# Mixer B of a two-layer decoder: splitting the projections of its last unit by halves and merging its first half one head later

## The chip, the cores and the metric

The kernel runs on one core of one Trainium2 chip. The metric is the device time of one execution in microseconds (us); lower is better. The core has a matrix engine (TensorE, PE), a vector engine (VectorE, DVE), a scalar engine (ScalarE, ACT), GpSimd (POOL), and SyncE (SP), which here issues nearly all DMA transfers.

## What is computed

A decoder trunk on 1024 tokens and 1024 features, in float32. Layer 1 is a forgetting attention and a convolutional feed-forward net (FFN). Layer 2, which the change is about, is a dilated sliding-window attention ("mixer B") in three dilation groups of eight heads, merged by softmax weights, an output projection and a second FFN; a last norm ends it. The reference, cut to layer 2:

```python
q = (h @ b_w_q[bl]).reshape(B, S, B_N_GROUPS, B_HEADS_PER_GROUP, B_HEAD_DIM)
outs, lses = [], []
for g, (window, dil) in enumerate(B_GROUPS):        # dilations 1, 4, 16
    o_g, lse_g = dilated_branch(q[:, :, g], kv[:, :, 0, g], kv[:, :, 1, g], dil, slopes[g])
    outs.append(o_g)
    lses.append(lse_g)
alpha = jax.nn.softmax(jnp.stack(lses, axis=0), axis=0)
o = jnp.sum(alpha[..., None].astype(outs[0].dtype) * jnp.stack(outs, axis=0), axis=0)
x = x + o.reshape(B, S, B_OUT_WIDTH) @ b_w_out[bl]
h = rms_norm(x, ffn_norm_g[layer])
x = x + conv_ffn(h, ffn_w_up[layer], ffn_conv_w[layer], ffn_conv_b[layer], ffn_w_down[layer])
```

## The kernel before

Every float32 operand of a matmul is a pair: a rounded high part (`yh`, `wh`, written by ACT) and the rest (`yl`, `wl`, written by DVE by a subtraction). `mm3` makes three matmuls of each product (L116 to L118). Tokens are handled in two halves of 512; `hf` or `m` is the number of the half. Weights come by DMA into `wraw` (L89), ACT makes `wh` (L94), DVE makes `wl` (L95).

Mixer B has 12 units: for each of the four head pairs p = 0..3 the groups g = 2, 1, 0. A unit's attention (`attend_b`) goes over m = 0, 1 and the two heads j = 0, 1: scores on PE (L477, L478), a softmax whose first pass is on DVE (L257: it writes `t`, and the row minimum into `st`) and whose exponential is on ACT (L262), transposes (L234) into `tp`, copied as the pair `pt` by ACT and DVE, and the products with v (L247) into `po`, added into `og` by DVE (L272). `values` of one cell (m, j) stands behind `scores_b` of the next cell.

`weave` mixes a unit's attention with a filler: the v, q and k projections of the next unit (`tasks_b`), which are matmuls with nothing of the attention in them. The last unit (p = 3, g = 0; unit 11) has no next unit. Its filler is the output projection of half 0, `out_proj`, and only from the moment on at which half 0 has been merged and stands in `yh`, `yl` (`placed`).

The merge of the three groups needs the softmax statistics of all three with tokens on the partitions. Group 0's are there already, in `st`. For the others `spread` transposes `st` on PE (L536) and stores the rows to DRAM (L548): for group 1 in four DMAs of 1024 separate 4-byte elements each. `stats_by_token` reads them back into `stats` (L599, two DMAs). With both, `each_half(m)` of unit 11 computes the weights (`weigh`: L560 `mn`, L561, L563, ACT L564, then L566 to L569), spreads them over features by PE (L616), scales and adds the groups (`merge_b`: L625 to L627) and splits the sum into `yh`, `yl` (`out_half`).

At the start of unit 11, `reload` brings the merged halves of p = 0..2 from DRAM into `yh`, `yl` (L650, L651) and the residual stream into `xT` (L653): six plus eight DMAs of 256 KB for each half. Then `out_proj` adds into `xT` (L667), and the FFN of half 0 begins: squares and their sum (ACT L175, DVE L177 into `cg` for half 0, `T2h` for half 1), column sums on PE (L185), the norm (PE L198, DVE L207, which writes eight normed pieces), their split into `yh` and `yl` (L152, L153), and the up matmuls (L817).

The order of the work is not that of the program text: the kernel is built under `TileContext(nc, schedule_with_timeline_sim=True)`, a scheduler that orders each engine's instructions, the DMAs on SP's queue among them, by a simulated time. Each engine then runs its list in that order and waits at an instruction until its operands are there. SP's DMAs are dealt to eight lanes, and a DMA waits until the one eight earlier has landed.

Of the kernel before, what the change touches and what calls it, by code (L numbers as in the profile page):

```python
# [8 lines left out]
F32 = mybir.dt.float32  # L9
F32R = mybir.dt.float32r  # L10
# [6 lines left out]
P = 128  # L17
S = 1024
D = 1024
KD = D // P  # L20
KH = KD // 2
NB = S // P
H2 = 512
# [7 lines left out]
NG = len(DILS)  # L31
# [3 lines left out]
RATIO_B = 2.0  # L35
# [15 lines left out]
def trunk(ctx, tc, x, a_w_in, a_b_f, a_w_out, b_w_q, b_w_out, kv_norm_g, w_kv,  # L51
          mix_norm_g, ffn_norm_g, ffn_w_up, ffn_conv_w, ffn_conv_b, ffn_w_down,
          final_norm_g, out):
    nc = tc.nc
# [67 lines left out]
        sl = half(hf)  # L122
        yield from mm3(ps, [(w[k], (yh[:, k, sl], yl[:, k, sl])) for k in range(len(w))])

    def stream(tasks):

        w = None
        for i, (load, body) in enumerate(tasks):
            w = w or load()
            ahead = tasks[i + 1][0]() if i + 1 < len(tasks) else None  # L130
            yield from body(w)
            w = ahead

# [3 lines left out]

    def weave(main, filler, ratio, ready=lambda: True):

        due = 0.0  # L140
        done = False
        for c in main:
            due = due + c * ratio if ready() else 0.0
            while due > 0 and not done:
                f = next(filler, None)
                done = f is None
                due -= f or 0
        while not done:
            done = next(filler, None) is None

# [267 lines left out]
        d = DILS[g]  # L418
        return lambda t: t if d == 1 else t.rearrange("p (r t) -> p r t", r=d // 2)

    def project_v_b(vT, v, g, ptr, w, banks):
        for hf in range(2):
            src, dst = by_residue(g, hf)
            ps = banks(hf)
            yield from project(ps, w, hf)
            nc.scalar.copy(dst(vT), src(ps))
            yield 0
        for b4 in range(2):
            tp = ptr.tile([P, H2], F32, name="tp")
            for b in range(4):  # L430
                nc.tensor.transpose(tp[:, b * P:(b + 1) * P],
                                    vT[:, (4 * b4 + b) * P:(4 * b4 + b + 1) * P], ident)
            dst = v[:, 4 * b4:4 * b4 + 4]
            split(dst[:, :, :, 0:64], dst[:, :, :, 64:P],
                  tp.rearrange("p (b j d) -> p b j d", b=4, j=2))

    def project_q_b(heads, g, w, banks):
        for hf in range(2):
            src, dst = by_residue(g, hf)
            ps = banks(hf)  # L440
            yield from project(ps, w, hf)
            for j, (s1, m1, m2) in enumerate(heads):
                pj = src(ps[64 * j:64 * j + 64])
                nc.scalar.activation(dst(s1[0:64]), pj, AF.Copy, scale=-0.125)
                nc.vector.scalar_tensor_tensor(out=dst(s1[64:P]), in0=pj, scalar=-0.125,
                                               in1=dst(s1[0:64]).bitcast(F32),
                                               op0=ALU.mult, op1=ALU.subtract)
            yield 0

    def project_k_b(heads, g, w, banks):  # L450
        for hf in range(2):
            src, dst = by_residue(g, hf)
            ps = banks(hf)
            yield from project(ps, w, hf)
            for j, (s1, m1, m2) in enumerate(heads):
                split(dst(m1[0:64]), dst(m2[0:64]), src(ps[64 * j:64 * j + 64]))
            yield 0
        for s1, m1, m2 in heads:
            nc.vector.tensor_copy(m1[64:P], m1[0:64])
            nc.vector.tensor_copy(m2[64:P], m2[0:64])  # L460

    def scores_b(ap, psc, p, g, j, head, st, m):

# [22 lines left out]
            yield 4 * P  # L486
        return cell

    def attend_b(ap, ps_, p, g, heads, v, og, st, each_half):
        psc, ptr, pov = ps_  # L490

        def values(m, j, cell):
            js = slice(64 * j, 64 * j + 64)
            po = pov.tile([P, H2], F32, name="po")
            f = 4 * m
            if g == 0:
                opening = [(f, f), (f + 2, f + 2)]
                adding = [(f + 1, f + 1), (f + 3, f + 2)]
                banks = [opening, adding] + ([[(f - 1, f)]] if m else [])
            else:  # L500
                banks = [[(f + 2 * i, f + 2 * i), (f + 2 * i + 1, f + 2 * i)] for i in range(2)]
            for bi, bank in enumerate(banks):
                groups = [(kb, (q - f) * P, [cell.get((kb, q)), cell.get((kb, q + 1))])
                          for kb, q in bank]
                yield from transposed_pv(ap, ptr, po, lambda kb: v[:, kb, j],
                                         (bi == 0, bi == len(banks) - 1), groups)
            add_parts(in_order(g, og[js], m), residues(g)(po))
            if j:
                each_half(m)

        waiting = None
        for m in range(2):
            for j in range(2):
                cell = yield from scores_b(ap, psc, p, g, j, heads[j], st, m)
                if waiting:
                    yield from values(*waiting)
                waiting = (m, j, cell)
        yield from values(*waiting)
# [112 lines left out]
    placed = []  # L631
# [10 lines left out]
        for i, t in enumerate(parts):  # L642
            nc.sync.dma_start(o_sp[k, i][:, sl], t.bitcast(F32))

    def reload(xT, n):

        for hf in range(2):
            sl = half(hf)
            for k in range(n):
                nc.sync.dma_start(yh[:, k, sl].bitcast(F32), o_sp[k, 0][:, sl])  # L650
                nc.sync.dma_start(yl[:, k, sl].bitcast(F32), o_sp[k, 1][:, sl])  # L651
            for d in range(KD):
                nc.sync.dma_start(xT[:, d, sl], x_sp[d][:, sl])  # L653
# [6 lines left out]
                yield d  # L660
                d += 1

    def out_proj(w_out, hf, xT):
        def body(d, w):
            ps = pmm.tile([P, H2], F32, name="mm")
            yield from project(ps, w, hf)
            nc.vector.tensor_tensor(out=xT[:, d, half(hf)], in0=ps, in1=xT[:, d, half(hf)],  # L667
                                    op=ALU.add)
            yield 0
        return stream([(lambda d=d: load_cols(w_out, d * P), lambda w, d=d: body(d, w))  # L670
                       for d in range(KD)])

# [328 lines left out]
    with ExitStack() as st:  # L1003
        psc = pool(st, "psc", bufs=3, space=PSUM)
        ptr = pool(st, "ptr", bufs=2, space=PSUM)
        pov = pool(st, "pov", space=PSUM)
        ps_ = (psc, ptr, pov)
        hp_r = pool(right, "heads_ar", side="right")
        vp = pool(st, "va")
        NP = A_HEADS // 2  # L1010
        heads, vals = {}, {}
# [33 lines left out]
        with ExitStack() as s0:  # L1045
# [7 lines left out]
            with ExitStack() as s1_:  # L1053
# [69 lines left out]
                first = tokens_in(0)  # L1123
# [11 lines left out]
                second = tokens_in(1)  # L1135
# [72 lines left out]
        for u in range(NP):  # L1208
            if u == NP - 1:
                right.close()  # L1210
                xT = pool(right, "xA", side="right").tile([P, KD, S], F32, name="xT")
                reload(xT, u)
                filler = out_proj(a_w_out[0], 0, xT)
            v = [vals[u // 2, hf][u % 2] for hf in range(2)]
            weave(attend_a(ap, ps_, u, heads[u], v, u == NP - 1), filler, RATIO_A,
                  lambda: u < NP - 1 or (u, 1) in placed)
# [36 lines left out]
    with ExitStack() as st:  # L1253
# [26 lines left out]
        def tasks_b(i):  # L1280
# [3 lines left out]
            def banks(n):  # L1284
                def bank(hf):
                    if i == 0 and n + hf in (1, 2):
                        return psc.tile([P, H2], F32, name="sc")
                    return pmm.tile([P, H2], F32, name="mm")
                return bank

            def v(w):
                vT = vtp.tile([P, S], F32, name="vT")
                vals[i] = ap.tile([P, NB, 2, P], F32R, name="v", bufs=2)
                yield from project_v_b(vT, vals[i], g, ptr, w, banks(0))

            def q(w):
                hp = hp_l if i % 2 else hp_r
                heads[i] = [[hp.tile([P, S], F32R, name=f"{n}{j}") for n in ("s1", "m1", "m2")]
                            for j in range(2)]
                yield from project_q_b(heads[i], g, w, banks(1))  # L1300

            def k(w):
                yield from project_k_b(heads[i], g, w, banks(2))

            def by_halves(ws):

# [14 lines left out]
                     lambda: load_cols(wkv, base, gain=g_kv)]  # L1321
            if i == 0:
                return [(lambda: [ld() for ld in loads], by_halves), (lambda: True, end)]
            return list(zip(loads, (v, q, k))) + [(lambda: True, end)]

        by_token = []
        due = []
        filler = stream([t for i in range(len(units)) for t in tasks_b(i)])
        while next(filler) is not None:
            pass  # L1330
        for i, (p, g) in enumerate(units):
            last = i == len(units) - 1
            if g == 2:
# [38 lines left out]
            if last:  # L1372
                right.close()
                xT = pool(right, "xB", side="right").tile([P, KD, S], F32, name="xT")
                reload(xT, p)
                placed.clear()
                filler = out_proj(b_w_out[0], 0, xT)
            weave(attend_b(ap, ps_, p, g, heads[i], vals[i], ogs[g], st, each_half),
                  filler, RATIO_B, lambda: not last or (p, 1) in placed)

    with ExitStack() as st:
        for hf, fp, mm, y3 in after_mixer(st, 1, b_w_out[0], xT):
# [31 lines left out]
```

## Time and profile before

| | us |
|---|---|
| median of 3 runs | 2649.62 (2649.51 to 2653.08) |
| the profiled execution, its own time | 2652.28 |
| its span, first to last instruction | 2650.5 |
| PE busy in the span | 2571.4 (97%) |
| DVE busy in the span | 1949.0 (74%) |
| ACT busy in the span | 1336.9 (50%) |
| mean granted TensorE clock | 0.989 of full speed |

The profiled execution is 2.66 us above the median of the runs. Times in the trace count from the start of the span. The stretch that the change touches lies between about 1850 and 1960 us, from the end of unit 10 to the start of the second FFN. A busy time adds up what an engine executed; instructions overlap a little on DVE and ACT, so a group's mean duration is somewhat above the distance from one start to the next.

### The profile page before, as it was taken

What the parts mean: (1) busy time and instruction counts of PE and PEld (TensorE: products, weight loads), DVE (VectorE), ACT (ScalarE), POOL (GpSimd) and SP (SyncE); (2) the same over time, 40 slices, a digit from 0 to 9 for tenths busy, and PEclk for the clock granted to TensorE, in tenths of its full rate; (3) what the DMA queues carried; (4) which work ended last, traced back from release to release, by engine and by line L of the source; (5) the groups of instructions that cost most, each with busy time, mean ns of one, the idle gap of its engine ahead of it and who ended that gap; (6) DMA issues with size and microseconds to landing.
All of it is one profiled execution on the core that took longest, in us unless ns stands there. A gap on an engine that the chain in (4) does not pass through costs nothing.

```text
span 2650.5 us, 36941 instructions
## 1 busy us (share of the span) xinstructions
PE 2571.4 (97%) x12756; PEld 2146.7 (81%) x12756; DVE 1949.0 (74%) x3837; ACT 1336.9 (50%) x2825; POOL 535.7 (20%) x617
## 2 busy tenths in 40 slices
PE   7999999999999999999989999999889999999998
PEld 5898888787788888888778888888677888888887
DVE  6677777677976767778866666767698777777787
ACT  6555656554543434444445565656545444444444
POOL 0222222210112211212132122211011211211121
PEclk9999999999999999999989999999999999999999
DMA  5121211523111111111412323232621111121113
GB/s 185 50 65 49 58 50 50 203 72 108 40 54 50 48 56 48 55 57 44 141 48 33 60 55 58 57 58 56 146 87 48 50 54 49 56 60 52 48 48 116
DMA packets 287380, 180.51 MB, mean 68 GB/s; under 512 B 47728, under 2 KB 263512, under 8 KB 287192
## 3 DMA queue, kind: packets, MB, share of 16 engines
q1 hardware_dynamic: 287080, 178.12, 24.5%
q8 instruction: 101, 1.65, 0.3%
q14 instruction: 87, 0.71, 0.1%
q10 hardware_dynamic: 112, 0.02, 0.0%
HBM read 149.96 MB, written 23.94 MB: 66 GB/s over the span
## 4 chain that ended last, share of the span: by engine, by line
PE 84%; DVE 7%; DMA 4%; ACT 3%; issue 2%; SPq 1%; POOL 0%; POOLq 0%; ACTq 0%; DVEq 0%
PE up L817 30%; PE mm L117 13%; PE mm L116 13%; PE mm L118 13%; PE po L247 4%; PE tp L234 3%; DVE u L768 1%; PE sc L357 1%; DVE t L257 1%; PE sc L358 1%; DMA wb<-wt 1%; DMA stat<-srow 1%; PE up L116 1%; PE up L117 1%; PE up L118 1%
## 5 line engine op out<-in xcount | busy, mean ns | idle before, releaser
L116 PE MATMUL mm<-yh,wh 128*128 128x512 f32 x960 | 380.7, 397 | 8.8 <-ACT yh L152 6.0
L117 PE MATMUL mm<-yl,wh 128*128 128x512 f32 x960 | 381.3, 397 | 0.5 <-DMA yl<-o_sp 0.5
L118 PE MATMUL mm<-yh,wl 128*128 128x512 f32 x960 | 379.6, 395 | 0.0
L152 ACT CAST wh<-wraw 128x512 fp32r<-128x512 f32 x228 | 140.9, 620 | 353.3 <-PE up L817 306.5
L922 DVE TENSOR_TENSOR xT<-mm,xT 128x512 f32<-128x512 f32 x320 | 217.9, 684 | 106.1 <-PE mm L118 104.4
L153 DVE TENSOR_TENSOR wl<-wraw,wh 128x512 fp32r<-128x512 f32 x228 | 169.5, 749 | 150.3 <-ACT wh L152 150.0
L817 PE MATMUL up<-yh,wh 128*128 128x512 f32 x704 | 274.4, 390 | 0.9 <-ACT wh L152 0.9
L817 PE MATMUL up<-yl,wh 128*128 128x512 f32 x704 | 274.1, 389 | 0.0
L817 PE MATMUL up<-yh,wl 128*128 128x512 f32 x704 | 269.0, 389 | 0.0
L117 PE MATMUL mm<-ml,wh 128*128 128x512 f32 x576 | 225.3, 391 | 1.4 <-DVE ml L153 1.4
L116 PE MATMUL mm<-mh,wh 128*128 128x512 f32 x576 | 224.7, 390 | 0.0
L118 PE MATMUL mm<-mh,wl 128*128 128x512 f32 x576 | 223.9, 389 | 0.0
L116 PEld LDWEIGHTS mm<-yh,wh 128*128 128x128 f32 x960 | 181.0, 189 | 44.3 <-ACT yh L152 6.6
L118 PEld LDWEIGHTS mm<-yh,wl 128*128 128x128 f32 x960 | 181.5, 189 | 34.7
L247 PE MATMUL po<-pt,v 128*128 128x256 f32 x1040 | 197.0, 293 | 11.4 <-DVE pt L153 9.7
L117 PEld LDWEIGHTS mm<-yl,wh 128*128 128x128 f32 x960 | 181.5, 189 | 32.7 <-DMA yl<-o_sp 0.7
L153 DVE TENSOR_TENSOR pt<-tp,pt 128x128 fp32r<-128x128 f32 (+2 forms) x408 | 170.7, 433 | 48.3 <-ACT pt L152 43.6
L152 ACT CAST pt<-tp 128x128 fp32r<-128x128 f32 (+2 forms) x408 | 149.6, 382 | 109.5 <-PE tp L234 63.2
L247 PEld LDWEIGHTS po<-pt,v 128*128 128x128 f32 x1040 | 157.3, 192 | 31.5 <-DVE pt L153 13.0
L95 DVE TENSOR_TENSOR wl<-wraw,wh 128x512 fp32r<-128x512 f32 x176 | 129.8, 740 | 69.0 <-ACT wh L94 61.7
L801 POOL TENSOR_TENSOR sraw<-fraw 128x512 f32<-128x512 f32 x40 | 64.8, 1621 | 562.0 <-DMA fraw<-in_ffn_w_up_dram 360.9
L817 PEld LDWEIGHTS up<-yh,wh 128*128 128x128 f32 x704 | 132.1, 188 | 29.8 <-ACT wh L152 1.8
(352 smaller groups left out, 6079.9 us busy)
## 6 DMA issues: line engine op xcount, KB each, us to landing
wraw<-in_ffn_w_down_dram SPq DMA_DIRECT2D x104, 256.0 KB
fraw<-in_ffn_w_up_dram SPq DMA_DIRECT2D x88, 256.0 KB
wraw<-in_ffn_w_up_dram SPq DMA_DIRECT2D x88, 256.0 KB
wraw<-in_a_w_in_dram SPq DMA_DIRECT2D x60, 256.0 KB
wraw<-in_w_kv_dram SPq DMA_DIRECT2D x48, 256.0 KB
wraw<-in_a_w_out_dram SPq DMA_DIRECT2D x32, 256.0 KB
xT<-x_sp SPq DMA_DIRECT2D x32, 256.0 KB
wraw<-in_b_w_q_dram SPq DMA_DIRECT2D x24, 256.0 KB
```

The lines of the kernel that those rows point to most:

```text
L95: nc.vector.tensor_tensor(out=wl, in0=raw, in1=wh.bitcast(F32), op=ALU.subtract)
L116: nc.tensor.matmul(ps, ah, bh, start=(i == 0), stop=False)
L117: nc.tensor.matmul(ps, ah, bl, start=False, stop=False)
L118: nc.tensor.matmul(ps, al, bh, start=False, stop=(i == n - 1))
L152: nc.scalar.copy(h, src)
L153: return nc.vector.tensor_tensor(out=l, in0=src, in1=h.bitcast(F32), op=ALU.subtract).ins
L234: nc.tensor.transpose(tp[:, i * P:(i + 1) * P], c, ident)
L247: nc.tensor.matmul(po[:, col:col + 2 * P], v(kb), pt[:, hl, i * 2 * P:(i + 1) * 2 * P], start=(first and i == 0 and hl == 0), stop=(last a ...
L257: nc.vector.tensor_tensor_reduce(out=t[:, a:b], in0=sc, in1=m, scale=1.0, scalar=INIT if ci == 0 else nm[ci - 1], op0=ALU.add, op1=ALU.min ...
L801: nc.gpsimd.tensor_tensor(out=raw[n], in0=raw[a], in1=raw[b], op=op)
L817: nc.tensor.matmul(ps[bank], a[:, c], b[:, k], start=(start and k == 0 and i == 0), stop=(k == KH - 1 and i == 2), skip_group_check=True)
L922: nc.vector.tensor_tensor(out=xT[:, d, sl], in0=ps, in1=xT[:, d, sl], op=ALU.add)
```

## The change

Only unit 11 and what is woven into unit 10 and unit 11 are touched.

- The three projections of unit 11 are made by halves. Half 0 stays woven into unit 10; half 1 becomes the filler of unit 11's own first half. A marker `NEED` makes `weave` finish that filler ahead of the scores of m = 1.
- `each_half(0)` of unit 11, the merge of half 0, is called after the values of cell (1, 0); before, it was after those of (0, 1).
- `reload` brings half 0 at the start of unit 11 and half 1 behind the marker.
- `out_proj` loads its first weights ahead of its first matmul (`loads_first`), then yields `WAIT` until half 0 is placed.
- v of the second half is staged in a `wb` tile in place of `vT`; the duplicates of k are copied by halves (eight copies of 64x512 in place of four of 64x1024).

The diff, cut to this (lines in the changed file are 19 to 26 later in the functions concerned: L560 becomes L586, L548 L574, L599 L625, L616 L642, L653 L679, L257 L276, L153 L172, L272 L291):

```diff
     def weave(main, filler, ratio, ready=lambda: True):
-        due = 0.0
-        done = False
+        due, met, done = 0.0, 0, False
         for c in main:
+            if c is NEED:
+                while not met:
+                    met = next(filler) is NEED
+                continue
             due = due + c * ratio if ready() else 0.0
             while due > 0 and not done:
                 f = next(filler, None)
+                if f is WAIT:
+                    due = 0.0
+                    break
                 done = f is None
-                due -= f or 0
+                due -= 0 if f is NEED else f or 0
+                met += f is NEED
...
-            nc.vector.tensor_copy(m1[64:P], m1[0:64])
-            nc.vector.tensor_copy(m2[64:P], m2[0:64])
+            nc.vector.tensor_copy(m1[64:P, sl], m1[0:64, sl])
+            nc.vector.tensor_copy(m2[64:P, sl], m2[0:64, sl])
...
             add_parts(in_order(g, og[js], m), residues(g)(po))
-            if j:
+            if last and m > j:
+                each_half(0)
+            if j and m >= last:
                 each_half(m)
         waiting = None
         for m in range(2):
+            if last and m:
+                yield NEED
             for j in range(2):
...
+            if i == len(units) - 1:
+                ws = []
+                def first(f):
+                    def body(w):
+                        ws.append(w)
+                        yield from f(w, (0,))
+                    return body
+                def second(_):
+                    for f, w in zip((v, q, k), ws):
+                        yield from f(w, (1,))
+                return (list(zip(loads, map(first, (v, q, k)))) +
+                        [(lambda: True, f) for f in (end, second, end)])
...
+        def last_filler(rest, p):
+            yield from take(rest)
+            yield NEED
+            reload(xT, p, 1)
+            sums = out_proj(b_w_out[0], 0, xT, loads_first=True)
+            yield next(sums)
+            while (p, 1) not in placed:
+                yield WAIT
+            yield from sums
...
-                reload(xT, p)
+                reload(xT, p, 0)
                 placed.clear()
-                filler = out_proj(b_w_out[0], 0, xT)
-            weave(attend_b(ap, ps_, p, g, heads[i], vals[i], ogs[g], st, each_half),
-                  filler, RATIO_B, lambda: not last or (p, 1) in placed)
+                filler = last_filler(filler, p)
+            weave(attend_b(ap, ps_, p, g, heads[i], vals[i], ogs[g], st, each_half, last),
+                  filler, RATIO_B)
```

What the scheduler makes of it at three places (numbers behind a name tell buffers apart; `x4` is four in a row).

On DVE, around the first instruction of the merge of half 0, `mn<-st,stats`. Before:

```order
L257 ISA t_18747,st_17692<-sc_18744,bias_18736 128x256
L257 ISA t_18753,st_17692<-sc_18750,bias_18736 128x256
L257 ISA t_18759,st_17692<-sc_18756,bias_18736 128x256
L153 TENSOR_TENSOR pt_18764<-tp_18763,pt_18764 128x512
L257 ISA t_18796,st_17692<-sc_18793,bias_18791 128x256
L560 TENSOR_TENSOR mn_18846<-st_17692,stats_18131 128x8
L257 ISA t_18802,st_17692<-sc_18799,bias_18791 128x256
```

And of the change:

```order
L276 ISA t_18671,st_17692<-sc_18668,bias_18642 128x256
L479 COPY m11_18363<-m11_18363 64x512
L480 COPY m21_18364<-m21_18364 64x512
L586 TENSOR_TENSOR mn_18926<-st_17692,stats_18131 128x8
L291 TENSOR_TENSOR og1_18214<-po_18543,og1_18214 64x2x256
L172 TENSOR_TENSOR pt_18679<-tp_18678,pt_18679 128x512
L587 TENSOR_TENSOR mn_18926<-mn_18926,stats_18131 128x8
L276 ISA t_18787,st_17692<-sc_18784,bias_18782 128x256
L172 TENSOR_TENSOR pt_18697<-tp_18696,pt_18697 128x256
L276 ISA t_18819,st_17692<-sc_18816,bias_18782 128x256
L95 TENSOR_TENSOR wl_19127<-wraw_19125,wh_19126 128x512
```

The instruction that waits for `stats` stands ahead of the `pt` of cell (0, 0) and ahead of all softmaxes of m = 1 (buffers 18782 and up); before, it stood behind the last softmax of m = 0, that `pt` and one softmax of m = 1. Soon behind it now comes a `wl` of an output weight, `wraw_19125`.

On SP, from the DMAs of `xT` ahead of the stores of the statistics. Before:

```order
L653 DMA xT_18681<-x_sp_76 128x512 x3
L548 DMA stat3_83<-srow_18601 1024x1x1 x4
L653 DMA xT_18681<-x_sp_76 128x512 x3
L599 DMA stats_18131<-stat3_83 128x16x1 x2
L650 DMA yh_88<-o_sp_77 128x512
L651 DMA yl_89<-o_sp_77 128x512
L653 DMA xT_18681<-x_sp_76 128x512 x8
L89 DMA wraw_19140<-in_b_w_out_dram 128x4x128
```

And of the change:

```order
L679 DMA xT_18590<-x_sp_76 128x512 x11
L574 DMA stat3_83<-srow_18576 1024x1x1 x4
L676 DMA yh_88<-o_sp_77 128x512
L677 DMA yl_89<-o_sp_77 128x512
L625 DMA stats_18131<-stat3_83 128x16x1 x2
L676 DMA yh_88<-o_sp_77 128x512
L677 DMA yl_89<-o_sp_77 128x512
L679 DMA xT_18590<-x_sp_76 128x512 x5
L89 DMA wraw_19125<-in_b_w_out_dram 128x4x128
```

(Of the pairs of `yh` and `yl` each is shown once: before there are three behind `stats`; in the change two stand ahead of `stats` and one behind.) The stores stay behind most of the `xT` transfers, and the first output weight behind the reload is still behind all of it.

On ACT, where the weight that follows the reload is used. Before:

```order
L262 ACTIVATE t_18932,st_17692<-t_18932,st_17692 128x256
L152 CAST yh_88<-og0_18675 128x512
L152 CAST pt_19014<-tp_19013 128x512
L152 CAST pt_19032<-tp_19031 128x256
L564 ACTIVATE ew_19077<-ew_19077 128x3x8
L94 CAST wh_19141<-wraw_19140 128x512
```

And of the change:

```order
L171 CAST pt_18679<-tp_18678 128x512
L171 CAST pt_18697<-tp_18696 128x256
L281 ACTIVATE t_18671,st_17692<-t_18671,st_17692 128x256
L94 CAST wh_19126<-wraw_19125 128x512
L281 ACTIVATE t_18787,st_17692<-t_18787,st_17692 128x256
L171 CAST pt_18697<-tp_18696 128x128
L281 ACTIVATE t_18819,st_17692<-t_18819,st_17692 128x256
L590 ACTIVATE ew_18928<-ew_18928 128x3x8
```

Before, the cast of that weight stood behind the merged `yh` and all exponentials but few; now it stands ahead of the exponentials of m = 1 and of the merge's own (`ew_18928`).

## Rows read from the trace of the kernel before

**Rows 1.** The page: the span, and the busy time of the two busiest engines

```profile
span 2650.5 us, 36941 instructions
PE 2571.4 (97%) x12756; PEld 2146.7 (81%) x12756; DVE 1949.0 (74%) x3837; ACT 1336.9 (50%) x2825; POOL 535.7 (20%) x617
```

**Rows 2.** Windows of the stretch by stage; the first line names the columns

```profile
core 0: us, PE busy (x) PEld busy (x) DVE busy (x) ACT busy (x) POOL busy (x), PEclk, DMA share, GB/s
1858.24:1886.82 28.58, 20.36 (x113) 16.59 (x111) 14.63 (x38) 12.78 (x35) 1.69 (x5) 0.95 0.70 97
1886.82:1902.45 15.63, 11.88 (x59) 9.11 (x59) 13.06 (x51) 10.18 (x31) 1.19 (x4) 0.76 0.91 286
1902.45:1924.91 22.46, 22.44 (x109) 18.76 (x110) 18.66 (x40) 11.47 (x24) 0.00 (x0) 1.00 0.33 98
1924.91:1954.30 29.39, 22.11 (x103) 17.90 (x101) 26.90 (x46) 20.18 (x35) 3.15 (x2) 0.91 0.46 141
1954.30:1959.72 5.42, 5.03 (x11) 3.38 (x11) 5.42 (x11) 0.13 (x1) 4.68 (x1) 0.55 0.00 0
```

**Rows 3.** Waits in 1850 to 1990: us in total, times, longest

```profile
DVE mn L560 <- DMA stats<-stat: 7.7, 1, 7.7
PE po L247 <- DVE pt L153: 7.5, 1, 7.5
PE up L817 <- DVE yl L153: 7.3, 1, 7.3
```

**Rows 4.** The chain that ended last: start, us, what

```profile
1866.60 15.56 DMA stat<-srow
1882.24 4.49 DMA stats<-stat
...
1895.83 4.05 DMA wraw<-in_b_w_out_dram
```

**Rows 5.** Timeline of SP's DMA issues: start, us, line, transfer, count

```profile
1860.09 9.09 SPq L548 DMA_DIRECT2D stat<-srow  x4
1869.22 7.05 SPq L653 DMA_DIRECT2D xT<-x_sp  x3
1882.24 3.44 SPq L599 DMA_DIRECT2D stats<-stat  x2
...
1889.21 5.53 SPq L653 DMA_DIRECT2D xT<-x_sp  x8
1895.15 1.73 SPq L89 DMA_DIRECT2D wraw<-in_b_w_out_dram  x3
```

**Rows 6.** DMA in 1448 to 1476, 40 slices of 0.7 us, and its statistics stores

```profile
GB/s 256 31 0 0 0 0 0 2 2 3 2 2 1 2 1 1 1 1 1 2 0 0 0 7 74 43 44 41 40 59 20 38 77 296 58 217 135 0 0 30
...
1451.45 6.49 SPq L548 DMA_DIRECT2D stat<-srow  x4
```

**Rows 7.** Timeline of PE: start, us, line, tiles, count, idle before and its releaser

```profile
1858.24 0.27 PE L536 MATMUL sc<-ident,st 128*32 128x128 f32 x1
...
1902.47 0.73 PE L116 MATMUL mm<-yh,wh 128*128 128x512 f32 x2 [0.18 <-ACT yh L152]
...
1954.95 0.63 PE L817 MATMUL up<-yh,T3l 128*128 128x512 f32 x1
1955.38 0.63 PE L817 MATMUL up<-yh,T3h 128*128 128x512 f32 x1
```

**Rows 8.** Timeline of DVE: durations, and distances from start to start

```profile
1875.71 1.08 DVE L272 TENSOR_TENSOR og<-po,og 64x512 f32<-64x512 f32 x1 [0.70 <-ACT og L271]
...
1877.03 0.42 DVE L257 CUSTOM_DVE_ANT_0 t<-sc,bias 128x256 f32<-128x256 f32 x1
...
1877.38 0.42 DVE L257 CUSTOM_DVE_ANT_0 t<-sc,bias 128x256 f32<-128x256 f32 x1
...
1878.07 0.69 DVE L153 TENSOR_TENSOR pt<-tp,pt 128x512 fp32r<-128x512 f32 x1
1878.67 0.41 DVE L257 CUSTOM_DVE_ANT_0 t<-sc,bias 128x256 f32<-128x256 f32 x1
```

More of the change, by code (lines that the diff above doesn't have):

```diff
@@ L123, in project, with take, stream @@
         yield from mm3(ps, [(w[k], (yh[:, k, sl], yl[:, k, sl])) for k in range(len(w))])
-    def stream(tasks):
+    NEED, WAIT = object(), object()
+    def take(gen):
+        for c in gen:
+            if c is None:
+                return
+            yield c
+    def stream(tasks, loads_first=False):
         w = None
@@ L130, in stream @@
             ahead = tasks[i + 1][0]() if i + 1 < len(tasks) else None
+            if loads_first and i == 0:
+                yield 0
             yield from body(w)
@@ L419, in residues, with project_v_b @@
         return lambda t: t if d == 1 else t.rearrange("p (r t) -> p r t", r=d // 2)
-    def project_v_b(vT, v, g, ptr, w, banks):
-        for hf in range(2):
+    def project_v_b(vT, v, g, ptr, w, banks, hfs=(0, 1)):
+        for hf in hfs:
             src, dst = by_residue(g, hf)
@@ L427, in project_v_b @@
             yield 0
-        for b4 in range(2):
+        for b4 in hfs:
             tp = ptr.tile([P, H2], F32, name="tp")
@@ L435, in project_v_b, with project_q_b @@
                   tp.rearrange("p (b j d) -> p b j d", b=4, j=2))
-    def project_q_b(heads, g, w, banks):
-        for hf in range(2):
+    def project_q_b(heads, g, w, banks, hfs=(0, 1)):
+        for hf in hfs:
             src, dst = by_residue(g, hf)
@@ L448, in project_q_b, with project_k_b @@
             yield 0
-    def project_k_b(heads, g, w, banks):
-        for hf in range(2):
+    def project_k_b(heads, g, w, banks, hfs=(0, 1)):
+        for hf in hfs:
             src, dst = by_residue(g, hf)
@@ L457, in project_k_b @@
             yield 0
+        sl = slice(hfs[0] * H2, (hfs[-1] + 1) * H2)
         for s1, m1, m2 in heads:
-            nc.vector.tensor_copy(m1[64:P], m1[0:64])
-            nc.vector.tensor_copy(m2[64:P], m2[0:64])
+            nc.vector.tensor_copy(m1[64:P, sl], m1[0:64, sl])
+            nc.vector.tensor_copy(m2[64:P, sl], m2[0:64, sl])
     def scores_b(ap, psc, p, g, j, head, st, m):
@@ L487, in scores_b, with attend_b @@
         return cell
-    def attend_b(ap, ps_, p, g, heads, v, og, st, each_half):
+    def attend_b(ap, ps_, p, g, heads, v, og, st, each_half, last):
         psc, ptr, pov = ps_
@@ L643, in emit_o, with reload @@
             nc.sync.dma_start(o_sp[k, i][:, sl], t.bitcast(F32))
-    def reload(xT, n):
-        for hf in range(2):
+    def reload(xT, n, *hfs):
+        for hf in hfs:
             sl = half(hf)
@@ L661, in blocks_done, with out_proj @@
                 d += 1
-    def out_proj(w_out, hf, xT):
+    def out_proj(w_out, hf, xT, loads_first=False):
         def body(d, w):
@@ L670, in out_proj @@
         return stream([(lambda d=d: load_cols(w_out, d * P), lambda w, d=d: body(d, w))
-                       for d in range(KD)])
+                       for d in range(KD)], loads_first)
     PLAIN = 2
@@ L1211, in trunk @@
                 xT = pool(right, "xA", side="right").tile([P, KD, S], F32, name="xT")
-                reload(xT, u)
+                reload(xT, u, 0, 1)
                 filler = out_proj(a_w_out[0], 0, xT)
@@ L1289, in banks, with v, q, k @@
                 return bank
[L1291 to L1303, printed above, removed]
+            def v(w, hfs=(0, 1)):
+                if hfs[0]:
+                    vT = ap.tile([P, NG, H2], F32, name="wb", bufs=2) \
+                        .rearrange("p g t -> p (g t)")
+                else:
+                    vT = vtp.tile([P, S], F32, name="vT")
+                    vals[i] = ap.tile([P, NB, 2, P], F32R, name="v", bufs=2)
+                yield from project_v_b(vT, vals[i], g, ptr, w, banks(0), hfs)
+            def q(w, hfs=(0, 1)):
+                if not hfs[0]:
+                    hp = hp_l if i % 2 else hp_r
+                    heads[i] = [[hp.tile([P, S], F32R, name=f"{n}{j}")
+                                 for n in ("s1", "m1", "m2")] for j in range(2)]
+                yield from project_q_b(heads[i], g, w, banks(1), hfs)
+            def k(w, hfs=(0, 1)):
+                yield from project_k_b(heads[i], g, w, banks(2), hfs)
             def by_halves(ws):
```

## The prediction, made before the changed kernel was timed

> **What bounds the kernel now.** I began with the page. PE is busy 97% of the span and DVE 74% [rows 1], so over the whole PE is the bound and only stretches where PE stands still can be won. The windows by stage show that such a stretch lies where the change is. I count from X, the transpose of unit 10's statistics at 1858.24 [rows 7], to 1959.72, from where the second FFN runs without a gap. In these 101.48 us PE is busy 81.8 and DVE 78.7 [rows 2]; the reader should see that DVE is the busier of the two from 1886.82 to 1902.45 (13.06 of 15.63) and after 1924.91 (26.90 of 29.39, then all of 5.42). PE's idle time is there because it waits for DVE: the waits show two large stops of PE, 7.5 us for a `pt` and 7.3 us for the first `yl` of the FFN, and one of DVE, 7.7 us for `stats` [rows 3]. The chain shows what is behind the first: 15.56 us of the stores of the statistics and 4.49 us of their reading back, one behind the other [rows 4]. SP's timeline gives the times: stores issued from 1860.09 (X+1.9) to 1869.18, reading back issued at 1882.24 (X+24.0, call this S), `mn` at 1886.82 (X+28.6) [rows 2, 5].
>
> So after `mn` the end of the stretch is set by DVE's list and its waits. I make a ledger: time from X to the end of the stretch = DVE's work + DVE's idle time. Before it is 78.67 + 22.81; the idle time is 13.95 ahead of `mn`, then 2.57, 3.80, 2.49 and 0 [rows 2].
>
> **The change part by part.**
>
> *Work.* PE gets the same products. DVE's list is the same but for four more copies (eight of 64x512 for four of 64x1024). Bounded by nothing (half the length, twice the count) and by the step of a 512-column operation, 0.60 from one start to the next [rows 8], this is 0 to 2.4 us; the half-length copy is nearest to half of it, so I take 0.3 each, about +1: 79.7 us of DVE work. The half-unit of projections is moved, not saved: PE's busy time falls nowhere.
>
> *The filler ahead of the wait.* The 24 k, 2 q and 18 output matmuls of 512 columns and the attention beside them are about 15 us of PE work behind X, at 0.21 each for the matmuls (109 in 22.44 us [rows 2]). That is what the change was to lay over the first stop. It can't shorten the stop: what ends it is the landing of `stats`, and PE reaches the end of its filler at about X+15, well ahead of S.
>
> *The landing of `stats`.* The stores still stand on SP behind most of the `xT` transfers (11 in a row ahead of them, where before five were spread over two places), and wait for the lane of one of those. Before they began at X+1.9 and were down 22.1 us later [rows 5]. They are small but slow by themselves: the same stores of another pair, with hardly a load beside them, moved 1 to 3 GB/s for 13 slices of 0.7 us, up to about 1462, some 11 us behind the start of their issue at 1451.45 [rows 6]. I bound S by X+13 (1.9 + 11) and X+25, and take X+24, that of the row with the same neighbours, since the stores again have a queue of 256 KB transfers ahead of them.
> The Trainium skill, "DMA: Bandwidth & Descriptors", section "Anatomy of one DMA — SWDGE (gpsimd path)", fits a DMA as about 2 us and a term by bytes, next to nothing for 4 KB. By that fit the stores would be down 2 us behind their issue, and the sum would be that of the rival "the cover works" below; the trace does not agree, with 13.1 us from the end of the issue at 1869.18 to 1882.24 [rows 5].
>
> *The first wait moves ahead in DVE's list.* That is the heart of it. The merge of half 0 is one head later in the program, yet its first instruction `mn` now stands ahead of the `pt` of cell (0, 0) and of every softmax of m = 1. Ahead of it DVE has behind X eight softmax passes at 0.34, six operations of 512 columns at 0.60, one add of 1.08 [rows 8], three short ones at some 0.2 and four half copies at 0.3: 9.2 us, with what it has in hand at X some 10.8, where before 14.63 were done [rows 2]. So DVE arrives at about X+12.5 and stands still for 16 us, not 7.7; with it every softmax, `pt` and exponential of m = 1, and PE behind these. `mn` itself comes at S + 4.6, X+28.6, as before; the work not done ahead of it lies behind it: 79.7 - 10.8 = 68.9 us, where before it was 64.0.
>
> *A second wait.* `wraw_19125`, an output weight, is on SP behind the rest of the reload, and its cast on ACT stands ahead of the exponentials of m = 1, its `wl` on DVE early behind `mn`. Reading back takes 3.44 of issue; the two transfers and five `xT` behind it go at 0.69 each (8 in 5.53); so it is issued at S+8.3, and lands 4.05 later [rows 4, 5], S+12.3; ACT's cast and so `wl` follow at about S+12.9, X+36.9. DVE would be there 3.1 us after `mn` (one add of 1.08, one operation of 0.60, four softmax-sized ones at 0.34), X+31.7. It waits 5.2 us. Between 0 (the weight lands with the reload's first pieces) and 8 I keep 5.2. Queued behind it are the softmaxes of m = 1 on DVE and three exponentials and the merge's own on ACT.
>
> *Other idle time of DVE* behind `mn` was 8.86 (2.57 + 3.80 + 2.49). Where DVE stands, ACT and PE catch up, so some of it goes. Bounds: 2.5 and 8.9; I take 5.5.
>
> *The stop at the FFN.* The column sums and norm of half 0 come sooner after the last output sum, and twelve up matmuls can start. But behind these PE waits for the squares of half 1 (`T2h`), at the end of the same DVE list; the 7.3 us stop moves a few matmuls on. I give it nothing of its own; the ledger holds it.
>
> *Ahead of X* PE has two more projection matmuls and three transposes, less four of v: +0.4. *Clock.* After the first stop the granted clock is 0.76 over the next 15.63 us, after the second 0.55, a matmul then taking 0.43 in place of 0.21 [rows 2, 7]; 11 of them cost about 2.4. A longer stop makes one more such start; most of it lies beside DVE's work. Between 0 and 2.4 I take 1.
>
> *Sum.* 28.6 (to `mn`) + 68.9 + 5.2 + 5.5 = 108.2 against 101.5: +6.7; with 0.4 and 1: **+8.1**. The profiled execution took 2652.28, so 2660.4 on it; it stands 2.66 above the median of the runs, so about **2657.7** against that median.
>
> **Rivals.**
>
> *One wait only.* The weight lands early, or DVE's order leaves slack: then 5.2 goes, and with the lower other idle time 3 more: -0.1 to +2.9. For it: three weights are loaded ahead now, and DVE's time there is a sum of small things. Against: SP's order puts the load behind the reload. 2649.5 to 2652.5, no change that can be told.
>
> *The stores land sooner.* With S at X+13 to X+20 all moves ahead by 4 to 11: -3 to +4, 2646.6 to 2653.6. For it: rows 6 show 11 us where little else is loaded. Against: rows 5 show 22.1 us with a load like that of the change.
>
> *The cover works, and it is faster.* Were the four stores down as soon as they are issued, at X+11 (1.9 + 9.09) or, unloaded, X+8.4 (1.9 + 6.49) [rows 5, 6], `mn` would come at X+13 to X+15.6, just when DVE gets there. With 14 for it the ledger gives 14 + 68.9 + 5.2 + 5.5 = 93.6, or -6.5 with the 0.4 and 1: 2643.1; without the second wait 2637.9. It decides from S below about X+10, or X+16 if the second wait goes too. For it: the order on PE does lay 15 us of filler there. Against it: the 15.56 us of the chain in which nothing but the stores is waited for [rows 4].
> It is also what the page of the Trainium skill named above would give.
>
> *Longer.* Other idle time stays at 8.9, and the second weight in line waits too: +12 to +14, 2661.5 to 2664.
>
> **How the numbers follow.** The forecast (both waits, 2654.5 to 2661) has 0.50, longer 0.10, one wait 0.17, sooner 0.12, cover 0.11. The range from 2647 to 2664 takes in the bounds of the single costs, and leaves out most of the cover case and the ends of the others. A measurement of this kernel tells from no change about 0.2%, 5.3 us, so 2644.3 and 2654.9. Slower by more: the forecast but for its lowest end, and longer, 0.58. Faster by more: most of the cover, with a little for a sum that is wrong elsewhere, 0.12. The same: 0.30.
>
> **What would show it.** Right: DVE's wait for `stats` at `mn` of 15 to 17 us from about X+12.5; a wait of ACT or DVE for an output weight of some 5 us soon after; the output projection going on at X+54 (before X+44.2, at 1902.47 [rows 7]); a stop of PE of some 6 us after the first twelve up matmuls. Wrong, if the reading back is issued before X+20, if DVE's idle time from X on stays under 25 us, or if PE has no stop at the FFN at all: then the ledger's work behind `mn` is not what ends the stretch.

## The result, and the profile after

The change is slower: its time is 1.006 of the kernel before (95% interval 1.0047 to 1.0073), 12 to 19 us. The median is 2667.98 us (2663.82 to 2668.84, 4 runs) beside 2650.46 (4 runs); the profiled execution took 2668.41, with a span of 2666.6. I had predicted 2657.7, and 2664.0 as the upper end. The direction and the places were right, the size was not.

The same stages as in [rows 2], by windows of the changed kernel (columns as there; the transpose X is at 1857.50 here, and the last row is what follows the end of the stretch):

```profile
1857.50:1886.46 28.96, 16.33 (x97) 14.27 (x95) 11.65 (x34) 11.59 (x31) 1.67 (x4) 0.83 0.72 116
1886.46:1917.11 30.65, 18.72 (x94) 15.84 (x94) 19.48 (x69) 14.19 (x41) 1.50 (x5) 0.66 0.34 94
1917.11:1936.44 19.33, 19.19 (x85) 15.78 (x86) 18.37 (x32) 11.04 (x20) 0.00 (x0) 1.00 0.47 138
1936.44:1972.33 35.89, 25.61 (x118) 20.60 (x116) 32.52 (x53) 17.67 (x30) 7.26 (x3) 0.95 0.40 131
1972.33:1979.28 6.95, 6.95 (x22) 5.81 (x23) 0.83 (x5) 0.21 (x1) 0.00 (x0) 0.53 0.00 0
```

`mn` comes as long after X as before (28.96 for 28.58). The loss is in the second row: from `mn` to the split of the merged half 0 it takes 30.65 us, where before it took 16.24 (from 1886.82 to 1903.06, the end of the `yl` at 1902.45). The next stage wins 2.5 back (19.33 for 21.85), the one after is 1.1 longer (35.89 for 34.81).

The waits in 1850 to 2010 answer to [rows 3]:

```profile
ACT wh L94 <- DMA wraw<-in_b_w_out_dram: 24.0, 1, 24.0
...
PE po L266 <- DVE og L291: 16.1, 3, 14.0
DVE mn L586 <- DMA stats<-stat: 14.6, 1, 14.6
...
DVE wl L95 <- ACT wh L94: 8.5, 2, 7.7
PE mm L204 <- DVE T2h L196: 8.2, 1, 8.2
```

DVE waits twice, 14.6 us at `mn` and 7.7 us at the `wl` of an output weight. ACT stands for 24.0 us at the cast of that weight, from 1872.8, one us into DVE's first wait, to 1896.84, just ahead of the end of its second. The stop of PE at the FFN is still there, now behind twelve up matmuls. SP's timeline, beside [rows 5]:

```profile
1852.76 6.61 SPq L679 DMA_DIRECT2D xT<-x_sp  x11
1859.76 9.57 SPq L574 DMA_DIRECT2D stat<-srow  x4
...
1880.82 4.54 SPq L625 DMA_DIRECT2D stats<-stat  x2
...
1889.57 35.00 SPq L89 DMA_DIRECT2D wraw<-in_b_w_out_dram  x7
```

and the two instructions that the weight holds up, from DVE's timeline and from ACT's:

```profile
1897.49 0.69 DVE L95 TENSOR_TENSOR wl<-wraw,wh 128x512 fp32r<-128x512 f32 x1 [7.72 <-ACT wh L94]
```

```profile
1896.84 0.62 ACT L94 CAST wh<-wraw 128x512 fp32r<-128x512 f32 x1 [24.04 <-DMA wraw<-in_b_w_out_dram]
```

Reading back is issued at X+23.3. The weight is issued 8.75 us later and lands another 7.27 later. The seven transfers of 256 KB ahead of it were issued within 4.2 us (1885.41 to 1889.57); before, 14 were, over 9.4 us (1885.72 to 1895.15).

### The profile page after: what moved, and what is told of

It reads as the page before. It is cut to its first block, busy times and chain, and to the rows that moved or that the text cites. A ratio compares the mean times of both kernels' runs of the same rounds, so it can differ in the third digit from the quotient of the medians.

```text
span 2666.6 us, 36949 instructions
## 1 busy us (share of the span) xinstructions
PE 2570.8 (96%) x12756; PEld 2148.1 (81%) x12756; DVE 1951.5 (73%) x3841; ACT 1336.3 (50%) x2825; POOL 533.3 (20%) x617
## 4 chain that ended last, share of the span: by engine, by line
PE 82%; DVE 8%; DMA 4%; ACT 3%; issue 2%; SPq 1%; POOL 0%; POOLq 0%; ACTq 0%; DVEq 0%
PE up L843 30%; PE mm L117 13%; PE mm L116 13%; PE mm L118 13%; PE po L266 4%; PE tp L253 3%; DVE t L276 1%; DVE u L794 1%; PE sc L376 1%; DMA wb<-wt 1%; PE sc L377 1%; PE up L116 1%; DMA stat<-srow 1%; PE up L118 1%; PE up L117 1%
## 5 line engine op out<-in xcount | busy, mean ns | idle before, releaser
L171 ACT CAST wh<-wraw 128x512 fp32r<-128x512 f32 x228 | 140.8, 619 | 357.2 <-PE up L843 306.4
L172 DVE TENSOR_TENSOR wl<-wraw,wh 128x512 fp32r<-128x512 f32 x228 | 172.5, 762 | 150.8 <-ACT wh L171 150.8
L172 DVE TENSOR_TENSOR pt<-tp,pt 128x128 fp32r<-128x128 f32 (+2 forms) x408 | 170.8, 433 | 45.3 <-ACT pt L171 40.8
L94 ACT CAST wh<-wraw 128x512 fp32r<-128x512 f32 x176 | 108.3, 619 | 101.1 <-PE mm L117 59.9
```

Of the source, the lines that this page charges most:

```text
L94: nc.scalar.copy(wh, raw)
L171: nc.scalar.copy(h, src)
L172: return nc.vector.tensor_tensor(out=l, in0=src, in1=h.bitcast(F32), op=ALU.subtract).ins
```

## The experiments

Each gives the ratio to the kernel before with its interval; a change of 0.001 is 2.65 us.

**mn late.** The merge's weights are queued on DVE behind the newest softmax pass:

```diff
                 if last:
-                    out_half(p, ogs, last_weights(ap, psc, st, by_token[0], m), m)
+                    with tc.issue_after(newest[0].ins):
+                        ws = last_weights(ap, psc, st, by_token[0], m)
+                    out_half(p, ogs, ws, m)
```

> The change, with the weights of the merge of half 0 (the first instruction is mn, which waits for the statistics) queued on DVE behind the last softmax pass of the second half. Theory (two waits in DVE's and ACT's lists make the loss: mn too early, then the output weight behind the reload): DVE does the 4 us of softmax passes that stand behind mn while it waits, but ACT still waits for the output weight ahead of the exponentials, so only 3 to 6 us come back: 2661 to 2665, with DVE's wait for stats at 11 us or less and ACT's wait for the weight still over 15 us. Rival (the place of mn alone makes it): 10 us or more come back, 2657 or less. Rival (the halves of the projection cost it, not DVE's order): nothing comes back, 2667.

Measured: 1.0073 (1.0058 to 1.0088), nothing back, where the theory had 3 to 6 us. By its time this is the last rival's case, but the waits show another reason:

```profile
ACT wh L94 <- DMA wraw<-in_b_w_out_dram: 25.1, 1, 25.1
DVE wl L95 <- ACT wh L94: 24.6, 2, 23.9
```

The wait for `stats` is gone, as `mn` now comes at 1905.70, and DVE does no more for it: the cast of the weight is ahead of the exponentials on ACT and its `wl` ahead of the softmax passes on DVE, so DVE stands there for 23.9 us instead. Taken alone, the place of `mn` is worth nothing. That the halves of the projection are not the cost, as that rival has it, is seen from the last two runs below.

**Weights first.** `reload(xT, p, 1)` is traced behind `yield from sums`; the next output weight then stands on SP ahead of the stores.

> The change, with the reload of half 1 traced behind the output projection of half 0, so that the next output weights stand on SP ahead of most of it. Theory: ACT's wait of 24.0 us and DVE's of 7.7 us for the weight go, mn keeps its wait of 14 us or so: 5 to 8 us come back, 2659 to 2663. Rival (only the statistics count): under 2 us come back, 2665 to 2668.

Measured: 1.0038 (1.0023 to 1.0053), 5.8 us back, as the theory has it (the interval just overlaps with that of the change, 1.0047 to 1.0073). ACT's long wait for the weight is gone, and `mn` waits for `stats` alone:

```profile
PE po L266 <- DVE og L291: 17.1, 3, 15.0
...
DVE mn L586 <- DMA stats<-stat: 15.9, 1, 15.9
```

**Both.**

> Both edits at once: mn behind the last softmax pass, and the output weights ahead of the reload of half 1. Theory: the two losses together are nearly all of it, 12 to 18 us come back, 2649 to 2656, and PE has no stop over 8 us ahead of the output projection. Rival (the split itself costs, or the stop at the FFN): less than 10 us come back, over 2657.

Measured: 1.0019 (1.0009 to 1.0028), 11 us back, just below the 12 to 18 of the theory and above the 10 of the rival; the median, 2657.68, is over the theory's 2656. So the two edits together bring back some 11 of the 16 us, and 5 us stay. Now the late `mn` counts: its wait is 6.8 us (15.9 with the weights first alone).

```profile
PE mm L204 <- DVE T2h L196: 8.1, 1, 8.1
...
PE po L266 <- DVE pt L172: 7.4, 2, 7.2
DVE mn L588 <- DMA stats<-stat: 6.8, 1, 6.8
```

**Merge called early.** `each_half(0)` again behind the values of cell (0, 1), all else as in the change.

> The change, with the merge of half 0 called where it was before, after the values of cell (0, 1). The scheduler puts mn at the same place of DVE's list, 14 instructions ahead of what it was in the kernel before. Theory: the place of the call does not matter, since the order is made by what is ready; within 3 us of the change, 2664 to 2670. Rival (merging one head later makes the loss): 5 us or more come back, 2662 or less.

Measured: 1.0047 (1.003 to 1.0063). That is 3.4 us under the change, a little more than I allowed, but the intervals overlap. DVE's wait is of the same kind, at the same instruction:

```profile
1889.74 0.17 DVE L584 TENSOR_TENSOR mn<-st,stats 128x8 f32<-128x8 f32 x1 [15.67 <-DMA stats<-stat]
```

So most of the loss is not made by merging one head later. With the projections split, the scheduler puts `mn` early wherever the call stands.

**Stores first.** The transfers of `xT` are queued on SP behind the four stores (by `tc.issue_after` on the last of them), in the change alone and with both edits above.

> The change, with the transfers of xT queued on SP behind the four stores of the statistics (and so the next output weight ahead of both). mn stays at its place of DVE's list. If the stores take so long because some ten 256 KB transfers are in front of them, the reading back is issued at about X+13, DVE's wait for stats falls from 14.6 to 3 to 6 us, and with the second wait gone too the time is 2648 to 2654. If the stores are as slow by themselves, the reading back is issued after X+20, DVE waits over 11 us, and the time is that of the run with the weights first, 2658 to 2662.

> The run with mn late and the weights first, with the transfers of xT behind the stores as well. If the load in front of the stores is what makes them late, mn waits for nothing and the time is at or under the kernel before, 2644 to 2650; if the stores are slow by themselves, no more than 3 us under the run without this edit, 2654 to 2658.

Measured: 1.002 (1.0011 to 1.003), and 1.0006 (0.9997 to 1.0015) with both edits. SP's timeline of the first (X at 1858.30), and its wait:

```profile
1859.03 7.37 SPq L576 DMA_DIRECT2D stat<-srow  x4
1866.50 6.89 SPq L686 DMA_DIRECT2D xT<-x_sp  x2
1878.72 4.13 SPq L627 DMA_DIRECT2D stats<-stat  x2
```

```profile
DVE mn L588 <- DMA stats<-stat: 11.6, 1, 11.6
```

The reading back is issued at X+20.4, 19.7 us after the first store. It was 21.1 us in the change (1859.76 to 1880.82) and 22.1 in [rows 5], so the load ahead makes some 1 to 2.5 of it, and the stores of 4-byte elements stay slow. Three weights of 256 KB are still issued just ahead of them here and two `xT` transfers just behind, and no run with the stores is without loads beside them. Against the weights first alone this is worth 4.8 us (1.002 for 1.0038). The time, a median of 2656.06, lay between my two cases, the wait with the second. In the version with both edits `mn` still waits 2.7 us for `stats`, and the gain, 3.4 us (1.0006 for 1.0019), is a little over the 3 that I gave the second case. In both pairs the intervals overlap.

**Statistics by PE.** The stores and loads of group 1's statistics are replaced, for the last head pair, by 16 matmuls (32 instructions in the trace) with a 0/1 matrix `perm` (row t has its one in column 4t+3) and one ACT copy:

```diff
+        for b in range(4):
+            for q in range(4):
+                nc.tensor.matmul(ps[:, 8 * b:8 * b + 8], perm[:, b * P + 3 - q:(b + 1) * P + 3 - q],
+                                 st[:, 1, 8 * q:8 * q + 8], start=(q == 0), stop=(q == 3))
+        nc.scalar.copy(r[:, 1].rearrange("t m (a b) -> t m a b", b=4),
+                       ps[:, :32].rearrange("t (b m a) -> t m a b", b=4, m=2))
```

It was put into the change, into the kernel before, and into the change with the reload of half 1 behind the output projection.

> The change, with the statistics of group 1 of the last head pair brought onto token partitions by 16 small PE matmuls with a 0/1 matrix and one ACT copy, in place of the transpose, the four stores of 4-byte elements and the two loads. Theory (the landing of stats is what the order of the change exposes): DVE's wait of 14.6 us at mn is gone, and the reload is no longer behind the stores, so the weight lands earlier too; 20 us or more come back against the change: 2640 to 2650, at or under the kernel before. Rival (PE and DVE are short of other work anyway, and the stop at the FFN grows by what is won): 2653 to 2660.

> The kernel before, with the same replacement of the stores and loads of group 1's statistics by PE matmuls. Theory: the wait of DVE for stats (7.7 us) and the stop of PE (7.5 us) go, and 4 to 8 us of it arrive at the end: 2643 to 2648. Rival (the filler of the last unit is too short, so PE stops anyway a little later): within 3 us of the kernel before.

> The change with the statistics by PE and also the reload of half 1 traced behind the output projection. Theory: with no stores ahead of it the weight is early in both, so this is within 3 us of the run with the statistics by PE alone. Rival (the second wait is independent of the stores): 5 us or more faster than that run.

Measured: the change with it 0.9977 (0.9967 to 0.9987), the kernel before with it 0.9996 (0.9987 to 1.0005), the third 0.9978 (0.9969 to 0.9987), the same as the first, as its theory has it. This is the experiment that decides: with the statistics there in time, the change turns from 16 us slower to 6 us faster. Both waits are gone: no wait of ACT for an output weight is left among that run's long ones, DVE waits 1.1 us at a `wl`, and `mn` waits for nothing:

```profile
1876.15 0.36 DVE L586 TENSOR_TENSOR mn<-st,stats 128x8 f32<-128x8 f32 x1
...
1895.88 0.68 DVE L172 TENSOR_TENSOR yl<-og,yh 128x512 fp32r<-128x512 f32 x1
```

The second line is the split of the merged half 0, at 1895.88; before it was at 1902.45. The kernel before gains nothing measurable by the same means; here my theory was wrong and the rival right. `mn` came at 1882.47 in place of 1886.82, but PE then stops at the FFN twice, in sum 9.3 us in place of 7.7 (7.34 and 0.39):

```profile
1948.91 0.80 PE L827 MATMUL up<-yl,T3h 128*128 128x512 f32 x1 [4.03 <-DVE yl L153]
...
1959.14 1.87 PE L185 MATMUL mm<-ones,T2h 128*128 128x1 f32 x8 [5.25 <-DVE T2h L177]
```

`T2h` is summed at 1959.14, where before it was 1959.78. Of the 4.35 us by which `mn` is earlier 0.6 are left there; 1.6 of the rest are the longer stops at the FFN.

**What of the change wins.** Statistics by PE, with the merge called early; and the same with the reload in one go and no weight loaded ahead. In the second the reload overwrites `yh` and `yl` of half 1 before the last unit is projected from them, so it projects other numbers with the same work; it is for its time only.

> The run with the statistics by PE (0.9977 of the kernel before), with the merge of half 0 called where the kernel before calls it. If the gain of that run over the kernel before with the same statistics (0.9996) comes from the halves of the projection, the ratio stays within 0.001 of 0.9977; if it comes from the later merge, it goes to about 0.9996.

> Of the change only the halves of the projection are left, with the statistics by PE: the merge is called early, the reload is made in one go at the start, and no output weight is loaded ahead of the placed half. If the halves of the projection alone make the gain, the ratio is 0.9967 to 0.9987; if the reload by halves or the weights ahead have a part in it, it is above 0.9987.

Measured: 0.9966 (0.9953 to 0.9979) and 0.9964 (0.995 to 0.9978), both a hair on the fast side of what was expected. The halves of the projection are what wins: against the kernel before with the same statistics (0.9996) the second is 8.5 us faster, and in the traces the sums of `T2h` come 8.2 us earlier (1950.96 for 1959.14). The later merge, the reload by halves and the weights ahead show no gain, though the reload by halves is needed for the halves of the projection to be right. The first of the two has the lowest time of the versions that compute the right numbers; it is faster than both kernels, and its interval overlaps with those of the other two with the statistics by PE.

## Why the prediction was wrong

**What held.** The first wait: predicted 16 us from X+12.5, measured 14.6 from X+14.4, since `mn` stands ahead of the softmaxes of m = 1 in DVE's list. The landing: reading back was taken at X+24 and came at X+23.3. The second wait is where it was said to be. PE's filler did end long before `stats` landed, so it could not shorten the stop. The output projection went on at 1915.25, X+57.8, for a predicted X+54. The case "the cover works" had the right sign: the change with the statistics by PE, where they come early, is faster. That it measured -6.1 (0.9977 of 2650), near the -6.5 of that case, is luck: the -6.5 holds a second wait of 5.2, which that run does not have, and without it the case says 2637.9, or -11.7. The case did not come about in the change because the stores took 21.1 us there, and still 19.7 with the `xT` transfers behind them. The Trainium skill, "DMA: Bandwidth & Descriptors", section "Anatomy of one DMA — SWDGE (gpsimd) path", fits a DMA that GpSimd issues with about 2 us and a term by bytes. The stores here are issued by SP, so the prediction took that fit beyond what it is for; the four stores of single 4-byte elements took 19.7 us.

**What failed is the size of three terms of the sum**, each in the same direction; no single one makes up the 8 us:

| term | predicted, us | measured, us | difference |
|---|---|---|---|
| up to X (X was at 1858.24) | +0.4 | -0.7 | -1.1 |
| X to `mn` | 28.6 | 28.96 | +0.4 |
| DVE's work from `mn` to the end of the stretch | 68.9 | 70.4 | +1.5 |
| second wait, on DVE | 5.2 | 7.7 | +2.5 |
| DVE's other idle time | 5.5 | 7.8 | +2.3 |
| behind the end of the stretch (the clock) | 1 | 3.5 | +2.5 |

The work is 19.48 + 18.37 + 32.52 of the windows; the idle time is 15.5, of which 7.7 is the second wait. Of the work, four instructions of the second FFN on DVE (`mh` and `ml`, L733, some 2.4 us) now stand ahead of the last `T2h`, where before they stood behind it (L707, from 1959.65); other parts went both ways. The last row is the profiled time, 16.1 longer, less 12.6 by which the stretch ends later (1972.33 for 1959.72). The differences sum to 8.1, as 8.1 + 8.1 = 16.2.

- *The second wait.* The step took the landing of the weight as 4.05 us behind its issue, from [rows 4], where 14 transfers ahead had been issued over 9.4 us. It was 7.27 here, with seven issued in 4.2 us just ahead. It also took the wait as something that adds to the first; the runs show more. With `mn` moved away the whole of the loss remained (1.0073), because ACT and DVE then met the weight's wait alone. With the weight moved away 5.8 us came back, with both 11. Two waits one behind the other in the same lists cover each other, and only the pair can be priced.
- *Other idle time.* "Where DVE stands, ACT and PE catch up" was wrong for ACT: it stood for 24.0 us at the same weight, so every exponential of m = 1 came late. Beside the second wait DVE's idle time is 3.45, 0.96 and 3.37 us in the three stages behind `mn` (before 2.57, 3.80 and 2.49): only the middle one fell. In the first of them DVE waits in turn for PE and ACT, and the granted clock is 0.66 (before 0.76).
- *The stop at the FFN.* I said it moves behind twelve matmuls and gave it nothing of its own; the slow start behind it I took at 1, as most of it would lie beside DVE's work. It does not: the slow start moves with the stop. Before, the stop was for `yl`, and the eleven matmuls at a granted clock of 0.55 lay ahead of the last sum, beside DVE's work [rows 2, 7]; from the sum to the next matmul it took 0.91 us:

```profile
1959.78 1.05 PE L185 MATMUL mm<-ones,T2h 128*128 128x1 f32 x8 [0.39 <-DVE T2h L177]
1960.69 0.48 PE L817 MATMUL up<-yh,T3h 128*128 128x512 f32 x1
```

In the change the stop is for `T2h`, and the slow start comes behind the sum, where PE is the bound:

```profile
1960.81 0.39 PE L843 MATMUL up<-yl,T3h 128*128 128x512 f32 x1
1961.04 0.39 PE L843 MATMUL up<-yh,T3l 128*128 128x512 f32 x1
...
1972.33 1.87 PE L204 MATMUL mm<-ones,T2h 128*128 128x1 f32 x8 [8.16 <-DVE T2h L196]
1974.06 0.77 PE L843 MATMUL up<-yh,T3h 128*128 128x512 f32 x1
1974.63 0.63 PE L843 MATMUL up<-yl,T3h 128*128 128x512 f32 x1
1975.06 0.63 PE L843 MATMUL up<-yh,T3l 128*128 128x512 f32 x1
1975.49 0.63 PE L843 MATMUL up<-yh,T3h 128*128 128x512 f32 x1
```

The matmuls follow each other at 0.43 after the stop, at half of full speed (1.2 for 2.4 GHz; the granted clock from 1972.33 to 1979.28 is 0.53), beside 0.23 ahead of it. Ten or eleven of them make 2.2 of the 3.5 us, and the sum, with 1.73 to the next matmul in place of 0.91, another 0.8. The last 0.5 I did not trace.

The rival "one wait only" was mispriced too, at +2.9 at most. With the second wait taken away the measured loss is still 1.0038, 10 us, of which the wait of 15.9 at `mn` in place of 7.73 is 8.

Left open: whether the later merge costs something. Two pairs of runs differ only in the place of its call, and in both the early call is a little faster (1.0047 and 1.006; with the statistics by PE 0.9966 and 0.9977), but the intervals overlap. The traces hold a reason: with the early call PE's long stop at the FFN is the one for `yl` again, as in the kernel before; so it is in the version with the statistics by PE:

```profile
1945.78 0.80 PE L851 MATMUL up<-yl,T3h 128*128 128x512 f32 x1 [7.32 <-DVE yl L172]
...
1951.19 1.86 PE L204 MATMUL mm<-ones,T2h 128*128 128x1 f32 x8 [0.35 <-DVE T2h L196]
```

With the later merge and the same statistics the two stops are 2.14 and 8.32 us.

## What to carry to other kernels

Read a moved order by its first instruction that waits for something slow, and ask what stands behind that in the same list. Work laid over a wait helps only where it is queued ahead of the waiting instruction, on every engine that the work needs; here PE's was and DVE's and ACT's was not. Two waits in one list are priced together, as taking away one may give nothing. Where cover seems worthless, look first whether the transfer can be had without DRAM: the same halves of the projection lost 16 us over the stores of 4-byte elements and won 6 to 9 us without them.

## What the runs showed of the hardware that I had not expected

The four stores of 1024 elements of 4 bytes each, to DRAM, took 19.7 us, from the first issue until the reading back could be issued, with three weights of 256 KB issued just ahead of them, 21.1 us in the change with eleven transfers of 256 KB ahead, and 22.1 in the kernel before [rows 5]. That is about 4.8 ns for each element (19.7 us over 4096), an average; no run varies the size or the number of the elements. I had read about 11 us as a lower bound out of the DMA rates in [rows 6], where the rate falls to zero some 11 us behind the first store. That is no sign of their end: with the stores first the rate falls in the same way, about 12 us behind the first store at 1859.03, while the reading back waits for the stores until 1878.72 (DMA in 1856 to 1884, 40 slices of 0.7 us):

```profile
GB/s 0 0 0 0 0 128 248 13 2 1 1 2 2 1 1 1 1 1 2 1 24 1 0 0 12 44 15 26 20 32 12 15 26 26 12 205 222 103 3 2
```

Sixteen matmuls of 128x8 and one copy did the same reordering on the chip.
